# Pairing expert places of unequal size: 128 with 32 and 64 with 32 slots, gathered in one product

## The chip, the core and the metric

The kernel runs on one core of a Trainium2 chip. The figure that counts is the device time of one execution, in microseconds (us). TensorE (PE) does the matrix products; VectorE (DVE) and ScalarE (ACT) read its results from PSUM and work on SBUF; GpSimd (POOL) does little here; SyncE (SP) issues the weight transfers, which 16 DMA engines carry from HBM into SBUF.

## The reference

A batch of 256 tokens of width 1024 passes two transformer blocks in fp32. What matters here is the end of the second one, a mixture of experts with 32 experts, of which each token uses 4:

```python
logits = t @ w_router + b_router                  # [256, 32]
top_val, top_idx = lax.top_k(logits, 4)
gate_w = softmax(top_val)
# for every expert e, over the tokens that chose it:
hb = xb @ w_exp_in[e] + b_exp_in[e]               # 1024 -> 2048
g  = minimum(hb[:, :1024], 7.0);  u = clip(hb[:, 1024:], -7.0, 7.0)
a  = g * sigmoid(1.702 * g) * (u + 1.0)
y_e = a @ w_exp_out[e] + b_exp_out[e]             # 1024 -> 1024
# y = sum over a token's experts of gate_w * y_e; out = layer_norm(ALPHA * h + y)
```

One expert has 3 x 1024 x 1024 fp32 weights, 12.6 MB; all 32 have 403 MB, and every one of them is read once.

## The kernel before

Up to 515 us of the profiled span the kernel does the first block, the attention of the second and the router. After that come the experts. They are worked off one after the other in 32 *places*. A place has a fixed number of token slots (128, 64 or 32, `SLOTS`, L27, read by `caps`), and on the chip the experts are sorted by the number of their tokens, so that the fullest get the places of 128 (`_places`, L1350). Experts 0 and 1 always take places 0 and 1, so that their weights can be fetched before the sort is known (`FIXED`). There are 4 places of 128 slots, 14 of 64 and 14 of 32.

Weights come in *tiles* of 2 MB, six to a place, four of the first matrix and two of the second. `Stream.ahead` (L61 to L73) issues them on SP's queue in the order of the places. A tile goes into one of nine buffers (`ring` 3, `halves` 3, `ring2`, `ring3`, `more4`), so SP waits with a tile until PE has read the tile nine before it. Transfers of one queue land in their order.

For each place (the loop at L1121), `hidden` multiplies the gathered tokens by the first matrix in four blocks (f = 0 to 3). The tokens are the stationary operand, the 512 weight columns stream past; where a place has 64 or 32 slots, two or four such products stand side by side in the array. `gated` turns a block round (by `ident`, or for 32 slots by `fold`, which adds up the four parts) and applies the activation on DVE and ACT. `out_rows` multiplies by the second matrix, `weigh` scales by the gate, and `scatter` adds the rows to the tokens' sums, which stay in four PSUM banks (`acc`).

Tokens are gathered for two places at a time: `gather(r0)` runs in pieces beside the odd place ahead of the pair (`todo`, L1124). `one_hots` makes, for both places and both halves of the tokens, a matrix of 128 columns that holds a one where a token sits in a slot, repeated 128/c times; the product of the tokens `hn` (stationary, 128 x 128) with the 2c columns of both places gives `xs` transposed. Both places of a pair have the same c. DVE copies the columns of the first place from PSUM, ACT those of the second, into one `xs` tile each, from three rotating buffers. A second small product (L1042) fetches gate and token number of every slot.

`sort_experts` runs in steps between blocks; `SORT` says at which (place, block). A scheduler sets the order on every engine from its own estimate of durations; the program's order is a preference only, apart from the stretches under `manual_schedule`.

Of the kernel before, what the change touches and what calls it, by code (L numbers as in the profile page):

```python
# [9 lines left out]
F32 = mybir.dt.float32  # L10
# [9 lines left out]
D = 1024  # L20
# [3 lines left out]
E = 32  # L24
K4 = 4
FIXED = 2
SLOTS = (64, 32, 32, 128, 32, 32, 128, 32, 32, 64, 64, 64, 64, 64, 64, 32)  # L27
RING = 3
HALVES = 3
TAIL = 7  # L30
SORT = ((0, 2), (0, 3), (3, 1), (18, 1), (20, 1))
NPRE = 11 + 4 + 3 * NU + 20 + 4 + 4
ALPHA = 2.0 ** 0.25
LAM_INIT = 0.2
# [89 lines left out]

def caps(r):

    return SLOTS[r // 2]


def build(nc, tc, ctx, a, dbg=None):  # L130
    V, A, T, G = nc.vector, nc.scalar, nc.tensor, nc.gpsimd
# [216 lines left out]
    with tc.manual_schedule(engines={ACT, DVE, mybir.EngineType.Pool}):  # L348
        for c in range(2):
# [5 lines left out]
            start = ws.cut_in(1024 * c + 512, 1024 * c + 1024)  # L355
# [13 lines left out]
    for c in range(2):  # L369
        p = proj_t(ps, ws.next(), xh, xl, step=8 if c else 4)  # L370
        if c == 0:
            r0 = []
# [13 lines left out]
    p = proj_t(ps, w, xh, xl, nm=1)  # L386
    V.tensor_tensor(ka, p[:, 0, :], rt, op=OP.mult)
    p = proj_n(ps, w, xh, xl, c0=128, cols=128)
# [24 lines left out]
    for nm in ("q", "k"):  # L413
        eo = []
        for i in range(2):
            p = proj_t(ps, ws.next(), xh, xl)
# [26 lines left out]
    for c in range(2):  # L443
        p = proj_n(ps, ws.next(), xh, xl)
# [65 lines left out]
    for c in range(2):  # L510
        p = proj_n(ps, ws.next(), xh, xl)
# [4 lines left out]
    for t in range(2):  # L516
        for h in range(4):
            i = t * 4 + h
# [48 lines left out]
    tmp, r = weighed(0, rowf, "r1")  # L567
    r1.append(r)
    summed(0, tmp)
    tmp, r = weighed(1, rowf, "r1")  # L570
# [70 lines left out]
    for t in range(2):  # L641
# [3 lines left out]
        tmp, r = weighed(t, row1, "r3")  # L645
# [21 lines left out]
    oh = act.tile([128, 8, 256], F32R, name="ah")  # L667
# [60 lines left out]
    for g in range(2):  # L728
        at = attention_pt(ps, w1, sa, (4 * g, 4 * g + 2))
        v_n(vB, g)  # L730
        b = ps.tile([128, 2, 2, 128], F32, name="b")
# [38 lines left out]
    mo = pool(ctx, "mo")  # L770
    hn = mo.tile([128, 2, D], F32, name="hn")
    iota = mo.tile([128, 264], F32, name="iota")
# [8 lines left out]
    gtok = mo.tile([128, 2, E, 2], F32, name="gtok")  # L781
# [29 lines left out]
    for c in range(2):  # L811
        wa, wb = ws.next(), ws.next()
        for mm in range(2):
            m = 4 * c + 2 * mm
# [30 lines left out]
    oneh = rp.tile([128, 2, K4, E], F32, name="oneh")  # L845
# [21 lines left out]

    def one_hots(r0, pos):

        c = caps(r0)  # L870
        oh = mo.tile([128, 2, 2, 128 // c, c], F32, name="oneh")
        for t in range(2):
            for i in range(2):
                last = V.tensor_scalar(oh[:, t, i], iota[:, None, 1:c + 1].to_broadcast([128, 128 // c, c]),
                                       pos[:, t, r0 + i:r0 + i + 1], None, op0=OP.is_equal)
        return oh, last

# [2 lines left out]
    for t in range(2):  # L880
# [7 lines left out]
        for k0 in (0, 4):  # L888
            p = ps.tile([128, 4, 128], F32, name="b")
# [11 lines left out]
        b = ps.tile([128, E], F32, name="b")  # L901
# [7 lines left out]
    last = chosen(1)  # L909
    for t in range(2):  # L910
        show(f"logits{t}", logits[:, t, :])
    b = ps.tile([128, 2, E], F32, name="b")
# [26 lines left out]
    em = pool(ctx, "em", 4, space=PSUM)  # L939
# [5 lines left out]
    scr = [acc[t][n] for t in range(2) for n in range(2)]  # L945

    def sort_experts():

        sp = mo
        b = scr[0][:, 0:2 * E].rearrange("p (i e) -> p i e", i=2)  # L950
        for i, (x, y) in enumerate(((sel, ones), (ones, sel))):
            for t in range(2):
                T.matmul(b[0:E, i, :], x[:, t, :] if i == 0 else x[:, 0:E], y[:, 0:E] if i == 0 else y[:, t, :],
                         start=t == 0, stop=t == 1)
        cn = sp.tile([E, E], F32, name="cn")
        V.tensor_copy(cn, b[0:E, 0, :])

        places = ep.tile([128, 128], F32, name="places", bufs=1)
        nc.gpsimd.dma_start(places, a["places"])
        bw = ep.tile([128, 512], F32, name="xs", bufs=3)  # L960
        nc.gpsimd.dma_start(bw, a["bin"])
        key = ep.tile([E, 7, E], F32, name="key", bufs=1)
        V.tensor_scalar(key[:, 0, :], b[0:E, 0, :], float(E), sortc[:, 0:1], op0=OP.mult, op1=OP.add)
        V.scalar_tensor_tensor(key[:, 1, :], b[0:E, 1, :], float(E), sortc[:, 2:2 + E], op0=OP.mult, op1=OP.add)
        V.tensor_tensor(key[:, 2:6, :], key[:, 0:1, :].to_broadcast([E, 4, E]), key[:, 1:2, :].to_broadcast([E, 4, E]),
                        op=OP.is_gt)
        b = scr[1][:, 0:2]
        T.matmul(b, key[:, 2:6, :].rearrange("p a e -> p (a e)"), ones[0:E, 0:2], start=True, stop=True)
        rank = sp.tile([128, 1], F32, name="rank")
        V.tensor_copy(rank, b[:, 0:1])  # L970
        perm = sp.tile([128, 4 * E], F32, name="perm")
        V.tensor_scalar(perm, places, rank, None, op0=OP.is_equal)
        V.tensor_copy(key[:, 6, :], sortc[:, 1:2].to_broadcast([E, E]))
        b = scr[2][0:E, 0:2 * E].rearrange("p (i e) -> p i e", i=2)
        T.matmul(b[:, 0, :], key[:, 6, :], perm[0:E, 0:E], start=True, stop=True)
        T.matmul(b[:, 1, :], cn, perm[0:E, 0:E], start=True, stop=True)
        V.tensor_copy(ids, b[:, 0, :])
        V.tensor_tensor(cn, b[:, 1, :], sortc[:, 2 + E:2 + 2 * E], op=OP.subtract)
        V.tensor_scalar(over, cn, 0.0, None, op0=OP.max)
        V.tensor_reduce(most, over, axis=AX.X, op=OP.max)  # L980
        b = scr[3][:, 0:128]
        T.transpose(b, pg.rearrange("p j t e -> p (j t e)"), ident)
        pgt = ep.tile([128, 128], F32, name="pgt", bufs=1)
        V.tensor_copy(pgt, b)
        b = scr[0][:, 0:4 * E].rearrange("p (j t e) -> p j t e", j=2, t=2)
        T.matmul(b.rearrange("p j t e -> p (j t e)"), pgt, perm, start=True, stop=True)
        V.tensor_copy(posm[:, :, FIXED:], b[:, 0, :, FIXED:])
        V.tensor_copy(gtok[:, :, FIXED:, 0], b[:, 1, :, FIXED:])
        yield
        b = em.tile([128, 4, 4, E], F32, name="m")  # L990
        for m in range(4):
            T.matmul(b[:, m].rearrange("p f e -> p (f e)"), bw[:, m * 128:(m + 1) * 128], perm, start=True, stop=True)
        for j in range(2):
            for i in range(2):
                V.tensor_scalar(bexp[:, FIXED:, :, j, i].rearrange("p e f -> p f e"), b[:, 2 * j + i, :, FIXED:],
                                float(j), None, op0=OP.add)
        yield

        bw = ep.tile([128, D], F32, name="xs", bufs=3)
        for t in range(2):  # L1000
            nc.gpsimd.dma_start(bw[64 + t * E:64 + (t + 1) * E, :], a["bout"])
        for n in range(2):
            for t in range(2):
                r = slice(64 + t * E, 64 + (t + 1) * E)
                T.matmul(acc[t][n], pgt[r, :], bw[r, n * 512:(n + 1) * 512], start=False, stop=False,
                         skip_group_check=True)

        for t in range(2):
            yield
            for n in range(2):  # L1010
                T.matmul(acc[t][n], aid, hn[:, t, n * 512:(n + 1) * 512], start=False, stop=False,
                         skip_group_check=True)
# [4 lines left out]
    ep = pool(ex2, "ep", 2)  # L1017

    def gather(r0):

        c = caps(r0)
        oh, _ = first if r0 == 0 else one_hots(r0, posm)
        xs = [ep.tile([128, 8, c], F32, name="xs", bufs=3) for _ in range(2)]
        for i in range(2):
            slots_of[r0 + i] = [xs[i]]
        per = min(8, 256 // c)
        for at, k0 in enumerate(range(0, 8, per)):
            b = (em.tile([128, 512], F32, name="m") if r0 else scr[at])[:, 0:per * 2 * c]  # L1030
            b = b.rearrange("p (k i c) -> p k i c", k=per, i=2)
            for kk in range(per):
                f = slice((k0 + kk) * 128, (k0 + kk + 1) * 128)
                for t in range(2):
                    T.matmul(b[:, kk], hn[:, t, f], oh[:, t, :, 0, :], start=t == 0, stop=t == 1)  # L1035
            for i in range(2):
                (A.copy if i else V.tensor_copy)(xs[i][:, k0:k0 + per], b[:, :, i, :])
            yield
        for i in range(2):
            b = em.tile([128, 2], F32, name="m")  # L1040
            for t in range(2):
                T.matmul(b, oh[:, t, i].rearrange("p d c -> p (d c)"), gtok[:, t, r0 + i, :],  # L1042
                         start=t == 0, stop=t == 1)
            gs = ep.tile([128, 2], F32, name="gs", bufs=5)
            V.tensor_copy(gs, b)
            V.tensor_scalar(gs[:, 0:1], gs[:, 0:1], 0.5, None, op0=OP.mult)
            so = ep.tile([128, 256], F32R, name="so", bufs=3)
            V.tensor_scalar(so, iota[:, 0:S], gs[:, 1:2], None, op0=OP.is_equal)
            slots_of[r0 + i] += gs[:, 0:1], so
# [65 lines left out]
    slots_of = {}  # L1115
# [5 lines left out]
    for r in range(E):  # L1121
        xs = slots_of[r][0]
# [304 lines left out]
```

## Time and profile before

| | us |
|---|---|
| timed runs of the kernel before | 1485.1, 1479.3, 1487.65 (median 1485.1) |
| the profiled execution, its own time | 1477.87 |
| its span | 1476.1 |
| granted TensorE clock, mean over the span | 0.978 |
| busy: PE, DVE, ACT | 1394.0 (94%), 657.4 (45%), 433.6 (29%) |

The page cuts the span into 40 slices of 36.9 us and shows a digit of busy share for each engine, the granted clock of TensorE, the share of the DMA engines and the bytes moved. PE's busy time is the time from the start of a product to its modelled end, so products that run beside one another or wait in the array for the one ahead count in full; PE at 9 in every slice does not mean that PE sets the pace there. The chain of waits on the page reaches back only to 1464 us, to the branch ahead of the final normalization, and tells nothing about the experts. For those one goes to the stretches, to the order of PE's work in time, and to what SP waits for.

### The profile page before, as it was taken

How to read it: one execution, taken by the hardware profiler on the slowest of the kernel's cores; microseconds unless marked ns; L12 is line 12 of the kernel's file. 1: busy time of each engine (PE TensorE's matmuls, PEld its weight loads, DVE VectorE, ACT ScalarE, POOL GpSimd, SP SyncE). 2: the span in 40 equal slices, each digit the busy share in tenths (PEclk: the TensorE clock that was granted, in tenths of full speed). 3: DMA queues.
4: the chain of work that ended last, by engine and by line, in shares of the span. 5: the costliest groups of instructions: out<-in, count | busy, mean ns of one | idle time of the engine just before them, and what ended most of it. 6: DMA issues, size and time to landing. Idle time of an engine off the chain costs nothing. (4 is left out here: it accounts for less than half of the span.)

```text
span 1476.1 us, 21068 instructions
## 1 busy us (share of the span) xinstructions
PE 1394.0 (94%) x8401; PEld 882.1 (60%) x8402; DVE 657.4 (45%) x1622; ACT 433.6 (29%) x819; POOL 36.7 (2%) x54
## 2 busy tenths in 40 slices
PE   7998999989999899999999899998999999999984
PEld 7988999979999744544545444454343443443431
DVE  5868977866667533222123221232332333233313
ACT  4535655544565212121112211122111111111111
POOL 1001000010001100000000000000000000000000
PEclk9999999999999999899999999999999999999987
DMA  8435545535435989999989999899999999999995
GB/s 350 172 129 184 215 172 199 203 137 200 179 142 197 392 328 365 427 427 426 427 349 418 426 427 426 349 417 427 426 426 428 426 427 426 427 426 427 426 427 213
DMA packets 38008, 495.15 MB, mean 335 GB/s; under 512 B 4561, under 2 KB 4881, under 8 KB 8593
## 3 DMA queue, kind: packets, MB, share of 16 engines
q1 hardware_dynamic: 35424, 486.69, 79.8%
q0 software_dynamic: 2192, 6.88, 1.4%
q8 instruction: 68, 1.11, 0.3%
q14 instruction: 36, 0.29, 0.1%
q10 hardware_dynamic: 288, 0.18, 0.0%
HBM read 492.68 MB, written 1.05 MB: 334 GB/s over the span
## 5 line engine op out<-in xcount | busy, mean ns | idle before, releaser
L1060 PE MATMUL m<-w,xs 128*64 128x512 f32 (+2 forms) x1392 | 315.2, 611 | 10.3 <-DMA w<-in_wexp_dram 10.3
L1077 DVE TENSOR_TENSOR gu<-m,bexp 128x256 f32<-128x256 f32 (+2 forms) x128 | 51.1, 399 | 457.2 <-PE m L1074 310.9
L1060 PEld LDWEIGHTS m<-w,xs 128*64 128x64 f32 (+2 forms) x1392 | 102.3, 136 | 167.9 <-issue 157.3
L1063 ACT COPY hs<-m 128x512 f32<-128x512 f32 x128 | 74.9, 585 | 416.0 <-PE m L1060 416.0
L232 PE MATMUL b<-ah,wh 128*128 128x256 f32 x1552 | 194.3, 282 | 1.4 <-ACT wh L83 1.4
L232 PEld LDWEIGHTS b<-ah,wh 128*128 128x128 f32 x1552 | 187.6, 191 | 3.3 <-ACT wh L83 1.8
L105 DVE TENSOR_TENSOR wh<-w,wh 128x1024 fp32r<-128x1024 f32 (+1 forms) x152 | 174.2, 1180 | 31.7 <-ACT wh L104 31.7
L104 ACT ACTIVATE wh<-w 128x1024 fp32r<-128x1024 f32 (+1 forms) x154 | 148.7, 1019 | 79.8 <-PE b L232 43.4
L1097 PE MATMUL m<-w,ea 128*32 128x512 f32 (+2 forms) x672 | 141.6, 614 | 9.3 <-DMA w<-in_wexp_dram 6.3
L1060 PE MATMUL m<-wh,xs 128*32 128x512 f32 (+2 forms) x656 | 121.4, 597 | 8.4 <-DMA wh<-in_wexp_dram 8.1
L205 DVE SCALAR_TENSOR_TENSOR one<-m,gs,one 128x512 fp32r<-128x512 f32 x64 | 46.8, 749 | 129.1 <-ACT one L204 127.7
L1084 ACT ACTIVATE th<-gu 128x128 f32<-128x128 f32 (+2 forms) x128 | 38.4, 300 | 215.3 <-DVE gu L1082 215.3
L232 PE MATMUL b<-al,wh 128*128 128x256 f32 x776 | 99.4, 280 | 0.0
L232 PEld LDWEIGHTS b<-al,wh 128*128 128x128 f32 x776 | 94.5, 190 | 0.0
L1097 PE MATMUL m<-wh,ea 128*64 128x512 f32 (+2 forms) x352 | 85.5, 627 | 4.9 <-DMA wh<-in_wexp_dram 4.1
L1097 PEld LDWEIGHTS m<-w,ea 128*32 128x32 f32 (+2 forms) x672 | 40.6, 129 | 78.4 <-issue 55.9
L1112 PE MATMUL acc<-one,so 128*128 128x512 f32 x256 | 77.5, 423 | 9.7 <-ACT one L204 8.6
L1072 PEld LDWEIGHTS m<-fold,hs 128*128 128x128 f32 x448 | 56.6, 196 | 48.0 <-issue 35.9
L1060 PEld LDWEIGHTS m<-wh,xs 128*32 128x32 f32 (+2 forms) x656 | 35.5, 124 | 72.4 <-issue 66.0
L1112 PEld LDWEIGHTS acc<-one,so 128*128 128x128 f32 x256 | 43.0, 188 | 50.0 <-ACT one L204 29.0
L1035 PE MATMUL m<-oneh,hn 128*128 128x64 f32 (+2 forms) x480 | 69.0, 299 | 0.0
L204 ACT ACTIVATE one<-m,gs 128x512 fp32r<-128x512 f32 x64 | 42.5, 686 | 82.1 <-PE m L1097 82.0
(370 smaller groups left out, 1384.5 us busy)
## 6 DMA issues: line engine op xcount, KB each, us to landing
w<-in_wexp_dram SPq DMA_DIRECT2D x128, 2048.0 KB, 37.4
wh<-in_wexp_dram SPq DMA_DIRECT2D x63, 2048.0 KB, 37.5
w<-in_wpre_dram SPq DMA_DIRECT2D x37, 2048.0 KB, 7.9
w<-in_wpre_dram SPq DMA_DIRECT2D x4, 512.0 KB, 7.9
w<-in_wexp_dram SPq DMA_DIRECT2D x4, 512.0 KB, 30.3
tab<-in_tab_dram SPq DMA_DIRECT2D x1, 1152.0 KB, 10.0
xn<-in_x_dram SPq DMA_DIRECT2D x2, 512.0 KB, 5.0
ra<-in_rowv_dram POOLq DMA_DIRECT2D x2, 512.0 KB, 7.2
```

The source lines that it names most:

```text
L104: self.nc.scalar.activation(h[:, c], t[:, c], AF.Copy)
L105: self.nc.vector.tensor_tensor(l[:, c], t[:, c], h[:, c].bitcast(F32), op=OP.subtract)
L204: return (A.activation(hi, src, AF.Copy, scale=scale), V.scalar_tensor_tensor(lo, src, scale, hi.bitcast(F32), op0=OP.mult, op1=OP.subtract))
L205: V.scalar_tensor_tensor(lo, src, scale, hi.bitcast(F32), op0=OP.mult, op1=OP.subtract))
L232: T.matmul(p[:, m, :], x[:, k, c], y[:, k, :], start=i == m == k == 0, stop=i == 2 and k == nk - 1, skip_group_check=True)
L1035: T.matmul(b[:, kk], hn[:, t, f], oh[:, t, :, 0, :], start=t == 0, stop=t == 1)
L1060: T.matmul(b[g * c:(g + 1) * c], xs[:, k, :], w[:, kk, :], start=k < n, stop=k >= 8 - n, skip_group_check=True)
L1063: A.copy(h, b)
L1072: T.matmul(p[:, j, :], h[:, j * 128:(j + 1) * 128], fold, start=True, stop=True)
L1077: V.tensor_tensor(both, p[:, :, 0:c], bexp[:, r, f].rearrange("p j i -> p (j i)")[:, :, None].to_broadcast([128, 4, c]), op=OP.add)
L1097: T.matmul(ys[n][g * c:(g + 1) * c], ac[:, kk, :], w[:, kk, n * 512:(n + 1) * 512], start=(j == kk == 0) if c == 128 else j < 64 // c, sto ...
L1112: T.matmul(acc[t][n], so[:, t * 128:(t + 1) * 128], y[:, n, :], start=first and y is yh, stop=last and y is yl, skip_group_check=True)
```

## The change

`SLOTS` now has one entry for each place. The list of sizes is the same (4 of 128, 14 of 64, 14 of 32), in another order:

```
before  64,64  32,32  32,32  128,128  32,32  32,32  128,128  32,32  32,32  six times 64,64  32,32
after   64,64  32,64  32,64  128,32  64,32  128,32  64,32  128,32  64,32  128,32  64,64  five times 64,32
```

Since the two places of a pair may differ, `one_hots` writes each place's matrix with its own c, and the gather takes the last c0 columns of the first and the first c1 of the second, which lie next to each other, as one streaming operand of c0 + c1 columns. Both places share one tile `xs`, which alternates between two names (`xs0`, `xs1`) with a buffer each. A PSUM bank is filled with as many 128-row blocks as fit (`per`: five of 96 columns, four of 128, three of 160) and copied by one instruction, on DVE and ACT in turn. In `sort_experts` the two bias tiles take these names, and the fetch and the use of the second one become two steps of `SORT`, at place 2, block 1 and block 3, where one step stood at place 3, block 1.

```diff
-SLOTS = (64, 32, 32, 128, 32, 32, 128, 32, 32, 64, 64, 64, 64, 64, 64, 32)
+SLOTS = ((64, 64, 32, 64, 32, 64) + 3 * (128, 32, 64, 32) + (128, 32, 64, 64) + 5 * (64, 32))
-SORT = ((0, 2), (0, 3), (3, 1), (18, 1), (20, 1))
+SORT = ((0, 2), (0, 3), (2, 1), (2, 3), (18, 1), (20, 1))
 def caps(r):
-    return SLOTS[r // 2]
+    return SLOTS[r]
...
-        c = caps(r0)
-        oh = mo.tile([128, 2, 2, 128 // c, c], F32, name="oneh")
+        oh = mo.tile([128, 2, 2, 128], F32, name="oneh")
         for t in range(2):
             for i in range(2):
-                last = V.tensor_scalar(oh[:, t, i], iota[:, None, 1:c + 1].to_broadcast([128, 128 // c, c]),
+                c = caps(r0 + i)
+                last = V.tensor_scalar(oh[:, t, i].rearrange("p (d c) -> p d c", c=c),
+                                       iota[:, None, 1:c + 1].to_broadcast([128, 128 // c, c]),
...
-        bw = ep.tile([128, D], F32, name="xs", bufs=3)
+        bw = ep.tile([128, D], F32, name="xs0", bufs=1)
         for t in range(2):
             nc.gpsimd.dma_start(bw[64 + t * E:64 + (t + 1) * E, :], a["bout"])
+        yield
...
-        c = caps(r0)
+        c0, c1 = caps(r0), caps(r0 + 1)
+        c = c0 + c1
-        xs = [ep.tile([128, 8, c], F32, name="xs", bufs=3) for _ in range(2)]
-        for i in range(2):
-            slots_of[r0 + i] = [xs[i]]
-        per = min(8, 256 // c)
+        xs = ep.tile([128, 8, c], F32, name=f"xs{r0 // 2 % 2}", bufs=1)
+        slots_of[r0], slots_of[r0 + 1] = [xs[:, :, 0:c0]], [xs[:, :, c0:]]
+        per = min(8, 512 // c)
         for at, k0 in enumerate(range(0, 8, per)):
...
-                    T.matmul(b[:, kk], hn[:, t, f], oh[:, t, :, 0, :], start=t == 0, stop=t == 1)
-            for i in range(2):
-                (A.copy if i else V.tensor_copy)(xs[i][:, k0:k0 + per], b[:, :, i, :])
+                    T.matmul(b[:, kk], hn[:, t, f], oh[:, t].rearrange("p i c -> p (i c)")[:, 128 - c0:128 + c1],
+                             start=t == 0, stop=t == 1)
+            (A.copy if at % 2 else V.tensor_copy)(xs[:, k0:k0 + n], b)
```

The lines of the changed kernel stand one or two further down than those of before (the product of `hidden` is L1060 before and L1061 after, that of `gather` L1035 and L1037). Two places in the order of PE show what moves.

First the place after the first 128. In the kernel before, PE goes from place 6 (128 slots) to place 7, also 128; `w`, `wh` are weight tiles, `xs` the gathered tokens, `ea` the activations, `oneh` the one-hot columns. An x8 counts instructions of the program; the trace has two records for each such fp32 product.

```order
L1097 MATMUL m<-wh_6336,ea 128x512 x4
L1060 MATMUL m<-wh_6392,xs 128x512 x8
L1097 MATMUL m<-wh_6336,ea 128x512 x4
L1060 MATMUL m<-w,xs 128x512 x8
L1074 MATMUL m<-ident,hs 128x128
```

In the changed kernel place 7 has 32 slots:

```order
L1098 MATMUL m<-wh_6340,ea 128x512 x4
L1061 MATMUL m<-wh_6406,xs_6290 32x512 x8
L1098 MATMUL m<-wh_6340,ea 128x512 x4
L1061 MATMUL m<-w,xs_6290 32x512 x8
L1073 MATMUL m<-fold,hs 128x32 x4
```

The blocks stand in the same order; those behind the 128 are now products of 32 slots, and the next 128 comes three places later.

Second, the gather for places 2 and 3, on PE beside place 1. Before:

```order
L1035 MATMUL m<-oneh,hn 128x64 x9
L1060 MATMUL m<-w,xs 64x512 x8
L1074 MATMUL m<-ident,hs 128x128 x4
L1042 MATMUL m<-gtok,oneh 128x2 x4
L1060 MATMUL m<-w_5361,xs 64x512 x8
L1074 MATMUL m<-ident,hs 128x128 x4
```

After:

```order
L1037 MATMUL m<-oneh,hn 128x96 x3
L1061 MATMUL m<-w,xs_5297 64x512 x8
L1075 MATMUL m<-ident,hs 128x128 x4
L1037 MATMUL m<-oneh,hn 128x96 x6
L1061 MATMUL m<-w_5358,xs_5297 64x512 x8
L1075 MATMUL m<-ident,hs 128x128 x4
L1044 MATMUL m<-gtok,oneh 128x2 x4
```

There are still 16 products for the pair. They are 96 columns wide where they were 64, and stand in two groups (of ten and six) with a block of `hidden` between them, where they stood in one.

## Rows read from the trace of the kernel before

**Rows 1.** The page: granted clock and bytes moved, in 40 slices of 36.9 us.
```profile
PEclk9999999999999999899999999999999999999987
GB/s 350 172 129 184 215 172 199 203 137 200 179 142 197 392 328 365 427 427 426 427 349 418 426 427 426 349 417 427 426 426 428 426 427 426 427 426 427 426 427 213
```
**Rows 2.** Stretches: us, busy time of each engine (x instructions), clock, DMA share, GB/s.
```profile
548.00:584.00 36.00, 36.00 (x206) 16.43 (x202) 11.22 (x40) 7.45 (x16) 1.00 (x2) 1.00 0.93 365
606.00:617.00 11.00, 11.00 (x50) 7.50 (x48) 0.42 (x1) 0.37 (x1) 0.00 (x0) 0.53 1.01 427
740.00:800.00 60.00, 60.00 (x319) 29.67 (x317) 16.23 (x56) 10.72 (x23) 0.00 (x0) 1.00 0.90 374
764.00:776.00 12.00, 12.00 (x62) 4.71 (x60) 2.98 (x8) 2.94 (x6) 0.00 (x0) 1.00 0.50 182
932.00:992.00 60.00, 60.00 (x359) 30.55 (x362) 20.14 (x78) 11.60 (x26) 0.00 (x0) 1.00 0.90 372
1052.00:1400.00 348.00, 336.81 (x1658) 141.30 (x1656) 113.39 (x377) 62.17 (x129) 0.00 (x0) 1.00 1.01 427
```
**Rows 3.** What SP's queue waited for from 744 to 780 us: total, times, longest.
```profile
SPq L69 <- PE m L1060: 22.9, 3, 12.2
SPq L69 <- PE m L1097: 17.6, 2, 10.8
```
**Rows 4.** PE in order of time, place 6: start, us, line, product [idle before].
```profile
691.25 7.03 PE L1060 MATMUL m<-w,xs 128*128 128x512 f32 x16
698.12 0.60 PE L1074 MATMUL m<-ident,hs 128*128 128x128 f32 x4
698.55 7.03 PE L1060 MATMUL m<-w,xs 128*128 128x512 f32 x16
```
**Rows 5.** PE in order of time, places 24 and 25, from scatter to scatter.
```profile
1224.70 2.46 PE L1112 MATMUL acc<-one,so 128*128 128x512 f32 x8
...
1243.78 1.94 PE L1097 MATMUL m<-wh,ea 128*64 128x512 f32 x8 [0.66 <-DMA wh<-in_wexp_dram]
...
1248.69 3.65 PE L1097 MATMUL m<-wh,ea 128*64 128x512 f32 x16 [0.52 <-DMA wh<-in_wexp_dram]
1252.27 2.44 PE L1112 MATMUL acc<-one,so 128*128 128x512 f32 x8
...
1283.11 2.22 PE L1112 MATMUL acc<-one,so 128*128 128x512 f32 x7
```
**Rows 6.** PE in order of time: first products of places 2 to 5, and one wait.
```profile
576.38 1.92 PE L1060 MATMUL m<-w,xs 128*32 128x512 f32 x16
...
595.28 1.49 PE L1060 MATMUL m<-w,xs 128*32 128x512 f32 x11
...
630.42 1.92 PE L1060 MATMUL m<-wh,xs 128*32 128x512 f32 x16
...
648.66 1.92 PE L1060 MATMUL m<-w,xs 128*32 128x512 f32 x16
651.59 1.92 PE L1060 MATMUL m<-wh,xs 128*32 128x512 f32 x16 [1.00 <-DMA wh<-in_wexp_dram]
```
**Rows 7.** PE in order of time: gathers of 64 and 128 columns, and a slow stretch.
```profile
606.86 7.09 PE L1035 MATMUL m<-oneh,hn 128*128 128x64 f32 x32
613.88 3.30 PE L1060 MATMUL m<-w,xs 128*32 128x512 f32 x16
...
736.08 3.68 PE L1035 MATMUL m<-oneh,hn 128*128 128x64 f32 x32
...
1268.52 1.95 PE L1035 MATMUL m<-oneh,hn 128*128 128x128 f32 x16
```
**Rows 8.** Groups by shape: out<-in xcount | busy us, mean ns | idle before.
```profile
L1063 ACT COPY hs<-m 128x512 f32<-128x512 f32 x128 | 74.9, 585 | 416.0 <-PE m L1060 416.0
L1035 PE MATMUL m<-oneh,hn 128*128 128x256 f32 x64 | 15.8, 389 | 0.0
L1077 DVE TENSOR_TENSOR gu<-m,bexp 128x512 f32<-128x512 f32 x16 | 11.1, 692 | 108.4 <-PE m L1074 108.4
```

More of the change, by code (lines that the diff above doesn't have):

```diff
@@ L959, in sort_experts @@
         nc.gpsimd.dma_start(places, a["places"])
-        bw = ep.tile([128, 512], F32, name="xs", bufs=3)
+        bw = ep.tile([128, 512], F32, name="xs1", bufs=1)
         nc.gpsimd.dma_start(bw, a["bin"])
@@ L1019, in gather @@
     def gather(r0):
-        c = caps(r0)
+        c0, c1 = caps(r0), caps(r0 + 1)
+        c = c0 + c1
         oh, _ = first if r0 == 0 else one_hots(r0, posm)
-        xs = [ep.tile([128, 8, c], F32, name="xs", bufs=3) for _ in range(2)]
-        for i in range(2):
-            slots_of[r0 + i] = [xs[i]]
-        per = min(8, 256 // c)
+        xs = ep.tile([128, 8, c], F32, name=f"xs{r0 // 2 % 2}", bufs=1)
+        slots_of[r0], slots_of[r0 + 1] = [xs[:, :, 0:c0]], [xs[:, :, c0:]]
+        per = min(8, 512 // c)
         for at, k0 in enumerate(range(0, 8, per)):
-            b = (em.tile([128, 512], F32, name="m") if r0 else scr[at])[:, 0:per * 2 * c]
-            b = b.rearrange("p (k i c) -> p k i c", k=per, i=2)
-            for kk in range(per):
+            n = min(per, 8 - k0)
+            b = (em.tile([128, 512], F32, name="m") if r0 else scr[at])[:, 0:n * c].rearrange("p (k c) -> p k c", k=n)
+            for kk in range(n):
                 f = slice((k0 + kk) * 128, (k0 + kk + 1) * 128)
                 for t in range(2):
-                    T.matmul(b[:, kk], hn[:, t, f], oh[:, t, :, 0, :], start=t == 0, stop=t == 1)
-            for i in range(2):
-                (A.copy if i else V.tensor_copy)(xs[i][:, k0:k0 + per], b[:, :, i, :])
+                    T.matmul(b[:, kk], hn[:, t, f], oh[:, t].rearrange("p i c -> p (i c)")[:, 128 - c0:128 + c1],
+                             start=t == 0, stop=t == 1)
+            (A.copy if at % 2 else V.tensor_copy)(xs[:, k0:k0 + n], b)
             yield
@@ L1041, in gather @@
             for t in range(2):
-                T.matmul(b, oh[:, t, i].rearrange("p d c -> p (d c)"), gtok[:, t, r0 + i, :],
-                         start=t == 0, stop=t == 1)
+                T.matmul(b, oh[:, t, i], gtok[:, t, r0 + i, :], start=t == 0, stop=t == 1)
             gs = ep.tile([128, 2], F32, name="gs", bufs=5)
```

## The prediction

> **What bounds the kernel now.** I read the slices of the page first. In the experts, from slice 17 on, the transfers run at 426 to 428 GB/s, and a few slices fall to 349 [rows 1]. That is the first thing to see: a flat ceiling with dents. 403 MB at that rate are 943 us, which is about the length of the stage, so the weight stream is the pace. The stretches confirm it: 427 GB/s over 348 us from 1052 us, and in two stretches of 60 us only 374 and 372 [rows 2]. One place, 12.58 MB, takes 12.58/0.427 = 29.5 us, one tile 4.9 us.
>
> The dents: (1 - 374/427) x 60 = 7.4 us of the stream are lost between 740 and 800 us, and (1 - 372/427) x 60 = 7.7 us between 932 and 992 [rows 2]; together 15.1 us. In the first of them SP waits for products, up to 12.2 us at a time, not for earlier transfers [rows 3]: all nine buffers are full, and PE is late in reading. Both dents follow the two pairs of 128-slot places (6 and 7, 12 and 13).
>
> Now PE's pace, place by place.
> - 128 slots: a block of `hidden` with no other work in it takes 698.12 - 691.25 = 6.87 us, the turn 0.43 us [rows 4]. `out_rows` has half as many products of the same shape. So 6 x 6.87 + 4 x 0.43 + 2.4 for the scatter [rows 5] = 45.3 us.
> - 64 slots: place 24, scatter to scatter, 27.57 us, less 1.18 us of waiting for weights = 26.4 us. Place 25, with a gather of 128 columns beside it, takes 30.8 us; the gather costs 4.4 us [rows 5].
> - 32 slots: place 4, 648.66 - 630.42 = 18.2 us [rows 6].
>
> Against 29.5 us, a 128 puts PE back by 15.8 us, a 64 brings 3.1 and a 32 11.3 us forward. Let the *lag* be the time by which PE starts a place after its first tile has landed. At 651.59 us PE waits for the second tile of place 5 [rows 6], which has just landed; the first landed 4.9 us earlier, at 646.7 us, so the lag of place 5 is 2.0 us. It is about 1 us at place 6, since place 5 with its gather is short of 29.5 us. Two 128s and the gather beside them (64 columns, 4.2 us by the rows below) cost 2 x 45.3 + 4.2 = 94.8 us against 59.0 us: at the end of place 7 the lag would be 37 us, and 7.4 us of it became a dent. The buffers hold about 29.5 us.
>
> **The change, part by part.** *Order of the places.* A cycle of 128, 32, 64, 32 costs PE 45.3 + 18.2 + 26.4 + 18.2 us and two gathers. The stream needs 117.9 us for it.
>
> *The gathers.* 64 columns take 3.68 us for 32 records, 128 columns 1.95 us for 16 [rows 7]: the same for each product. So 96, between the two, costs as much; with the small products behind it the gather is 4.2 us at 64 columns and 4.4 at 128, and I take 4.4. 256 columns take 7.9 us for 32 records (15.8 us for two pairs) [rows 8]. A pair of 160 columns lies between 3.9 and 7.9 us; I take 4.9 us, a quarter of the way, since 160 is a quarter of the way from 128 to 256. With the small products, 5.4 us. The cycle is then 108.1 + 4.4 + 5.4 = 117.9 us, level with the stream; 3 us more if 160 costs as much as 256, 1 us less if as little as 128.
>
> *The start of the run of cycles.* Backwards from place 5: place 4 took 18.2 us, so its lag was 2.0 + 29.5 - 18.2 = 13.3 us; place 3 took 35.1 us: 7.7 us; place 2 took 18.9 us [rows 6], and (1 - 365/427) x 36 = 5.2 us of the stream were lost beside the sort [rows 2]: 23.5 us. All this is untouched by the change. Place 3's 35.1 us contain 12.7 us beyond 18.2 + 4.2: the bias products of the sort and a stretch at half clock. I leave these 12.7 us in, whatever place they now fall in. Places 2 to 5 are then 18.9 + 12.7 + (26.4 + 4.4) + 18.2 + (26.4 + 5.4) = 112.4 us against 117.9 + 5.2, and the lag at place 6 is 23.5 + 112.4 - 123.1 = 12.8 us. After the 128 it is 12.8 + 45.3 - 29.5 = 28.6 us, just under the 29.5 us at which the stream stops. The three places behind it take it down to 12.8 us again, four times over. So both dents go, 15.1 us, and with a margin of 1 us something comes back: I take 2 us in all, between 0 and 10 us (a cycle 3 us over the stream four times, less the margin, gives 11).
>
> *The end.* Behind the last cycle come 64, 64 and five pairs of 64, 32: 26.4 + 18.2 + 4.4 = 49.0 us against 59.0 us. The lag is gone after two of them, and the last place has 32 slots in both kernels. The stream sets the end, and its gain is the kernel's.
>
> *Copies.* 58 copies of 256 columns become 36 of 288 to 512. The nearest rows, other reads of 512 columns out of PSUM, take 692 ns on DVE and 585 ns on ACT [rows 8]. They are needed one place later, 18 us away, and both engines are busy for less than a third of this stage [rows 2]: nothing. If that cover were gone, 3 x 0.7 us would stand in each pair's gather, at most 2 us a pair. Sharing a buffer between the places takes nothing away, since the tile that is overwritten belongs to the pair before the last one. *Sort.* The second bias fetch and its products come a place earlier, behind the same buffer; nothing, and if PE waited for the fetch, less than the 18.9 us of place 2, in a lag that would then cost that much at place 6. One transpose moves ahead of the first product: under 1 us, and the stream is stopped there by full buffers only later.
>
> *A rule against it.* From 606 to 617 us the granted clock is 0.53, that is mostly the lower level (1.2 GHz); PE was at work all the time [rows 2], on narrow products and on bias products with 32 rows. The Trainium skill (TensorE: Matmul & The Clock Gate, "HAM oscillation — how this bites in real kernels") says that a kernel whose matmuls wait for transfers between bursts falls back to the slow clock burst by burst. By it the last ten places, with 10 us of waiting in each pair, would run at half clock: a pair would take 2 x 49 = 98 us instead of 59, and the end would come 5 x 39 = 195 us later, near 1664 us. This case's trace does not bear that out: from slice 18 to slice 38 the clock digit is 9 (0.9 or more) throughout, though pairs of 32 wait longer than pairs of 64, 32 will [rows 1].
>
> The sum: 1477.9 - 15.1 + 2 = 1464.8 us for an execution like the profiled one. The median of the timed runs lies 7.2 us above that execution and the lowest 1.4 us; I carry 4 us, and predict 1469 us.
>
> **The rivals.** *The dents come back smaller.* PE's cycle is level with the stream by my sum, and 2 to 3 us more in each would fill the buffers behind every 128. For it: the margin of 1 us, and the unknown price of 160 columns. Against it: the 12.7 us at place 3 need not all return. Gain 3 to 9 us; profile 1472, predicted time 1476 us.
>
> *The stream is not on the path.* The weights come earlier, and PE, which now has no pause from place 6 to place 21, sets the end itself. For it: PE is at 9 in nearly every slice. Against it: from 1222 us PE waits 0.66 and 0.52 us for tiles [rows 5], so it is level with the stream twelve places before the end, and the new order leaves 10 us more in each of the last pairs. No change: 1482 us.
>
> *Slower: the half clock.* At 606 us the gather takes 7.09 us instead of 3.68 and a block 3.30 us instead of 1.92 [rows 6, 7]: 4.8 us for one stretch. If it came in both 32s of a cycle, where narrow products, scatter and gather meet, a cycle would be 9.6 us longer; four of them, less the 1 us of margin, stop the stream for 37 us against 15.1 us removed. It turns against the kernel at 4 us a cycle. With one stretch a cycle: 18 us against 15, with two, 22 us lost. I price it between them, 12 us on 1477.9 + 4: 1494 us. (The rule's own case, 1664 us, gets 0.01 of this rival's chance.) For it: the stretch came with PE busy. Against it: behind slice 17 the clock digit stays at 9 through ten places of 32 slots, up to slice 38 [rows 1].
>
> **How the numbers follow.** The forecast (gain 9 to 16 us) 0.62, the smaller dents 0.20, no change 0.10, the half clock 0.08. What a measurement of this kernel can tell from no change is 0.5%, 7.4 us of 1485.1. Faster: 0.62, and two fifths of the smaller dents, 0.08, make 0.70. Slower: the half clock and a little of no change, 0.10. The rest, 0.20, is the same. The range for eight in ten: from 1459 us (15.1 us off the profiled execution with nothing coming back is 1462.8, less 4 us for the spread of the runs) to 1486 us (no change, with the median's excess).
>
> **What would show it.** Right: slices at 426 from 600 us on, SP waiting for transfers and not 10 us for products behind a 128, and pairs of 96 columns at 3.7 to 4 us for 32 records. Smaller dents would show as 10 us waits of SP at places 8, 12, 16 and 20. The stream is not on the path if PE has no waits for weights after 1250 us. The half clock is in the clock row. My lags are wrong if PE waits for weights between places 6 and 20.

## The result, and the profile after

The changed kernel takes 1467.0 us (median of 4 runs, 1466.1 to 1467.3), the kernel before 1482.4 us (median of 4, 1479.3 to 1487.7) beside it. The ratio is 0.989 with an interval of 0.986 to 0.993. The profiled execution of the changed kernel took 1467.0 us, with a span of 1465.2 us; that of before had 1477.9 and 1476.1.

The page of the changed kernel has the same two lines as [rows 1], clock and bytes in 40 slices, here of 36.6 us; the third line is from its list of transfers (number of issues, KB each, median us from issue to landing).

```profile
PEclk9999999999999989999999999999999999999997
GB/s 351 175 93 179 225 208 174 178 178 203 162 146 150 393 313 373 425 426 427 427 426 428 426 428 426 426 426 427 426 427 427 426 428 424 428 427 426 425 428 204
w<-in_wexp_dram SPq DMA_DIRECT2D x128, 2048.0 KB, 27.3
```

The four slices of 349, 418, 349 and 417 are gone: from slice 17 to the last but one all stand between 424 and 428. The stretches that answer to [rows 2], with the same columns:

```profile
548.00:584.00 36.00, 36.00 (x202) 16.82 (x201) 13.15 (x47) 6.15 (x13) 1.01 (x2) 1.00 0.93 371
606.00:617.00 11.00, 11.00 (x66) 5.99 (x60) 3.85 (x9) 2.64 (x5) 0.00 (x0) 1.00 1.01 426
740.00:800.00 60.00, 58.70 (x380) 28.31 (x380) 20.25 (x78) 12.50 (x27) 0.00 (x0) 1.00 1.01 427
932.00:992.00 60.00, 58.75 (x277) 29.32 (x275) 17.33 (x55) 9.84 (x20) 0.00 (x0) 1.00 1.01 427
1052.00:1400.00 348.00, 325.58 (x1778) 146.34 (x1776) 101.32 (x350) 60.80 (x126) 0.00 (x0) 0.98 1.01 427
```

740 to 800 and 932 to 992 went from 374 and 372 to 427 GB/s. The stretch at 606 us, which had the clock at 0.53, has it at 1.00.

Next, PE in order of time (start, us, line, product, idle time before it and what ended it): the first products of places 2, 6, 7, 8 and 10, and two waits in the last places.

```profile
580.23 1.92 PE L1061 MATMUL m<-w,xs 128*32 128x512 f32 x16
...
686.27 13.89 PE L1061 MATMUL m<-w,xs 128*128 128x512 f32 x32
...
725.89 1.92 PE L1061 MATMUL m<-wh,xs 128*32 128x512 f32 x16
...
754.94 3.65 PE L1061 MATMUL m<-w,xs 128*64 128x512 f32 x16
...
804.90 5.31 PE L1061 MATMUL m<-wh,xs 128*128 128x512 f32 x12
...
1401.39 3.65 PE L1061 MATMUL m<-w,xs 128*64 128x512 f32 x16 [0.67 <-DMA w<-in_wexp_dram]
...
1425.90 1.92 PE L1061 MATMUL m<-w,xs 128*32 128x512 f32 x16 [1.93 <-DMA w<-in_wexp_dram]
```

A cycle of 128, 32, 64, 32 took 804.90 - 686.27 = 118.6 us, the second as long, the third 120.3 us. With the landing times of the first tiles, which the trace records, the lags come out at 6.7 us at place 6 and 6.2, 7.2 and 8.4 us at places 10, 14 and 18. From place 20, where it is 20.8 us, the lag falls to 0.3 us at place 26; from there on PE waits for weights, as in the two last rows. The stream sets the end.

The clean measure of the gain is the time from the first product of place 0 to the end of the span. The two rows are that product, before and after, each from its own trace.

```profile
522.90 3.65 PE L1060 MATMUL m<-w,xs 128*64 128x512 f32 x16
```

```profile
526.86 3.65 PE L1061 MATMUL m<-w,xs 128*64 128x512 f32 x16
```

Before: 1476.1 - 522.9 = 953.2 us. After: 1465.2 - 526.9 = 938.3 us. The experts became 14.9 us shorter, and the two dents had held 15.1 us.

### The profile page after: what moved, and what is told of

It is laid out like the page before. It is cut to its first block, busy times and chain, and to the rows that moved or that the text cites. A ratio compares the mean times of both kernels' runs of the same rounds, so it can differ in the third digit from the quotient of the medians.

```text
span 1465.2 us, 21035 instructions
## 1 busy us (share of the span) xinstructions
PE 1386.9 (95%) x8401; PEld 878.4 (60%) x8402; DVE 659.4 (45%) x1613; ACT 429.9 (29%) x806; POOL 36.7 (3%) x54
## 5 line engine op out<-in xcount | busy, mean ns | idle before, releaser
L1061 PE MATMUL m<-w,xs 128*64 128x512 f32 (+2 forms) x1392 | 301.7, 600 | 10.7 <-DMA w<-in_wexp_dram 10.7
L1061 PEld LDWEIGHTS m<-w,xs 128*64 128x64 f32 (+2 forms) x1392 | 96.6, 133 | 167.9 <-issue 160.7
L1098 PE MATMUL m<-w,ea 128*32 128x512 f32 (+2 forms) x672 | 136.9, 625 | 8.2 <-DMA w<-in_wexp_dram 6.5
L1061 PE MATMUL m<-wh,xs 128*32 128x512 f32 (+2 forms) x656 | 127.8, 597 | 4.5 <-DMA wh<-in_wexp_dram 4.5
L1073 PEld LDWEIGHTS m<-fold,hs 128*128 128x128 f32 x448 | 55.6, 194 | 47.1 <-issue 36.9
L1061 PEld LDWEIGHTS m<-wh,xs 128*32 128x32 f32 (+2 forms) x656 | 39.2, 128 | 71.2 <-issue 68.3
L1037 PE MATMUL m<-oneh,hn 128*128 128x96 f32 (+2 forms) x480 | 64.2, 283 | 0.0
## 6 DMA issues: line engine op xcount, KB each, us to landing
w<-in_wexp_dram SPq DMA_DIRECT2D x128, 2048.0 KB, 27.3
```

What stands on the lines that cost most here:

```text
L1037: T.matmul(b[:, kk], hn[:, t, f], oh[:, t].rearrange("p i c -> p (i c)")[:, 128 - c0:128 + c1], start=t == 0, stop=t == 1)
L1061: T.matmul(b[g * c:(g + 1) * c], xs[:, k, :], w[:, kk, :], start=k < n, stop=k >= 8 - n, skip_group_check=True)
L1073: T.matmul(p[:, j, :], h[:, j * 128:(j + 1) * 128], fold, start=True, stop=True)
L1098: T.matmul(ys[n][g * c:(g + 1) * c], ac[:, kk, :], w[:, kk, n * 512:(n + 1) * 512], start=(j == kk == 0) if c == 128 else j < 64 // c, sto ...
```

## The experiments

Two questions were open. Is it the order of the places that brings the 15 us, or the joint gather with its fewer copies? And does the lag, measured against what the buffers hold, explain the dents, or would any order that mixes large with small do? Below, "stage" is the time from place 0's first product to the end of the span, 953.2 us before and 938.3 us after. In a SLOTS edit the removed line is that of the changed kernel.

**The joint gather with the old order (e1_old_order).**

```diff
-SLOTS = ((64, 64, 32, 64, 32, 64) + 3 * (128, 32, 64, 32) + (128, 32, 64, 64) + 5 * (64, 32))
+SLOTS = tuple(c for c in (64, 32, 32, 128, 32, 32, 128, 32, 32, 64, 64, 64, 64, 64, 64, 32) for _ in range(2))
```

> The joint product and the shared tile stay, the places stand in the order of the kernel before (pairs of equal size). Theory (the order of the places alone decides, through the lag of PE behind the weight stream and the nine buffers): both dents come back, 7 to 8 us of the stream lost at 740-800 us and again at 932-992 us, time near 1482 us. Rival (the gather in one product with fewer copies is what gains): no dents worth the name, 1467 us.

Measured: 1479.8 us against 1480.0 for the kernel before, ratio 0.9996 (0.9977 to 1.0015); the stage is 953.1 us. The two stretches in its trace:

```profile
740.00:800.00 60.00, 60.00 (x320) 29.80 (x318) 16.69 (x56) 10.06 (x21) 0.00 (x0) 1.00 0.90 373
932.00:992.00 60.00, 60.00 (x359) 30.56 (x362) 20.39 (x78) 11.23 (x25) 0.00 (x0) 1.00 0.90 372
```

Both dents are back, to within 1 GB/s. In the old order the rewritten gather is worth nothing, and so are its fewer copies; the gain comes with the new order. Whether that order needs the joint gather for it is the next question.

**The new order, each pair gathered in two products (e2_two_products).**

```diff
-                for t in range(2):
-                    T.matmul(b[:, kk], hn[:, t, f], oh[:, t].rearrange("p i c -> p (i c)")[:, 128 - c0:128 + c1],
-                             start=t == 0, stop=t == 1)
+                for x, y in ((128 - c0, 128), (128, 128 + c1)):
+                    for t in range(2):
+                        T.matmul(b[:, kk, x - 128 + c0:y - 128 + c0], hn[:, t, f], oh[:, t].rearrange("p i c -> p (i c)")[:, x:y],
+                                 start=t == 0, stop=t == 1)
```

> The order of the changed kernel, but each place of a pair is gathered by a product of its own, 32 products for a pair where there were 16. Theory: 32 products of 64 records take 64 x 0.115 = 7.4 us where 96 columns take 3.7 and 160 about 4.9, so a cycle of four places is 6 us over the stream; from a lag at the end of the first 128 of 22.5 + 6 = 28.7 us against 29.5 us that the buffers hold, the second, third and fourth 128 stop the stream for about 5, 6 and 6 us: 1467 + 17 = 1484 us, SP waiting for PE behind places 10, 14 and 18. Rival (PE's work is hidden behind the stream as long as the order is mixed): 1467 to 1470 us.

Measured: 1520.2 us, ratio to before 1.024 (1.019 to 1.028). Slower than before, as expected, but by 36 us more than expected. Its clock row, its first gather, its stretches and two moments with the clock low:

```profile
PEclk9999999999999799999999999999999996996998
...
520.86 13.89 PE L1038 MATMUL acc<-oneh,hn 128*128 128x64 f32 x64 [0.73 <-DVE oneh L874]
...
524.00:584.00 60.00, 60.00 (x310) 35.03 (x310) 16.76 (x63) 7.61 (x15) 0.00 (x0) 0.87 0.71 285
560.00:860.00 300.00, 296.49 (x1610) 147.61 (x1607) 85.41 (x289) 50.32 (x103) 1.01 (x2) 0.99 0.99 417
860.00:1160.00 300.00, 294.52 (x1583) 150.53 (x1583) 82.08 (x275) 49.12 (x100) 0.00 (x0) 0.99 0.94 391
1160.00:1460.00 300.00, 298.62 (x1612) 143.81 (x1612) 82.81 (x293) 48.98 (x103) 0.00 (x0) 0.89 0.99 414
...
1256.00:1280.00 24.00, 24.00 (x111) 14.92 (x111) 4.30 (x21) 2.08 (x5) 0.00 (x0) 0.50 0.93 384
1375.00:1402.00 27.00, 27.00 (x127) 16.35 (x126) 5.34 (x26) 2.34 (x6) 0.00 (x0) 0.51 1.01 426
```

The first gather takes 13.9 us where the changed kernel's takes 6.4, and place 0 starts 9 us later (the clock is at its lower level beside both, in e2 from 516 to 539 us at 0.50). Then the stream, which waits for buffers, loses 7.0, 25.3 and 9.1 us in the three long stretches (each (1 - GB/s / 427) x 300): 41.4 us, where the theory had 17. It had no term for the later start and none for the clock. At 1256 and 1375 us the clock is at its lower level for 24 and 27 us, with PE busy all the time. And all PE waited for from 560 to 1510 us were these two (total, times, longest):

```profile
PE acc L1114 <- ACT one L204: 8.7, 11, 0.8
PE m L1099 <- DVE ea L1090: 2.5, 6, 0.4
```

No transfer is among them: here PE sets the end, with a lag of 24 us still at the last place. So the new order with a product for each place loses; with the joint product, which keeps the gather at the price of one, it gains. How much of the 58.6 us between the two spans belongs to the doubled products and how much to the clock I can't separate, since the parts overlap.

**The four 128s, each with a 32, one behind the other (e3_wide_in_a_row).**

```diff
-SLOTS = ((64, 64, 32, 64, 32, 64) + 3 * (128, 32, 64, 32) + (128, 32, 64, 64) + 5 * (64, 32))
+SLOTS = ((64, 64, 32, 64, 32, 64) + 4 * (128, 32) + 3 * (64, 32) + (64, 64) + 5 * (64, 32))
```

> The changed kernel with the four pairs of 128 and 32 in a row, the three pairs of 64 and 32 behind them; all sizes and products are the same. Theory: each such pair costs PE 45.3 + 18.2 + 4.4 = 67.9 us against 59.0 us of the stream, the lag at the end of the 128s is 22.5, 31.4 and so on, capacity 29.5 us: the stream stops for 2, 9 and 9 us, 20 us in all, 1487 us. Rival (any mixing of sizes within a pair is enough): 1467 us.

Measured: 1492.7 us (1485.7 to 1496.2), ratio 1.007 (1.005 to 1.009); the stage is 1490.8 - 524.3 = 966.5 us, 28.2 longer than that of the changed kernel. The stretch and the page's row of bytes:

```profile
800.00:1000.00 200.00, 196.44 (x940) 97.48 (x940) 53.57 (x177) 32.00 (x65) 0.00 (x0) 0.97 0.92 371
...
GB/s 347 170 120 189 215 170 203 204 127 198 178 170 187 377 331 400 426 426 427 428 427 406 356 349 358 350 427 426 426 426 427 426 427 427 427 427 427 426 427 202
```

The pairs hold the same mix, yet (1 - 371/427) x 200 = 26.2 us are lost, more than in the kernel before. A pair of 128, 32 costs PE 68.9 us with its gather, against 59.0 us of the stream, and four of them in a row add up: the lags at the four 128s are 6.5, 17.2, 28.6 and 33.5 us, where the changed kernel has 6.7, 6.2, 7.2 and 8.4. (Two short stretches at half clock, at 819 and 890 us, add to it; they may be the 6 us beyond the expected 20.) It is the running sum that decides, not the mix within a pair.

**The changed kernel again, and with eight buffers in place of nine, in both kernels (e4_after_again, e5_eight_buffers_after, e6_eight_buffers_before).** e4 has no edit; e5 and e6 have this one, on the changed kernel and on the kernel before:

```diff
-    ws.free += ws.halves + [(pool(ctx, "more4"), "w")]
+    ws.free += ws.halves
```

> The changed kernel itself, as the yardstick for the runs beside it: 1467 us, ratio to the kernel before 0.99. Rival (a difference of chips or days): anything else.

> The changed kernel with eight weight buffers instead of nine. Theory: the lag that stops the stream falls from 29.5 to 24.6 us, and the largest lag at the end of a 128 is 6.7 + 45.3 - 29.5 = 22.5 us in the first three cycles and 24 us in the last: still no dents in the middle; only the start, where all buffers are full while the router works, loses one more tile, 5 us: 1472 us. Rival (any loss of buffering costs, the order has no margin): 1480 us or more.

> The kernel before with eight weight buffers instead of nine. Theory: one tile more at the start, and 4.9 us more in each of the two dents: 1480 + 5 + 10 = 1495 us, so that the distance to the changed kernel grows from 13 to 23 us. Rival (the dents are of another kind, such as the place's own latency): 1485 us, the same distance as with nine.

Measured, beside the kernel before at 1481.0 us: e4 1467.3 us, ratio 0.991 (0.989 to 0.993), stage 1463.4 - 525.0 = 938.4 us; e5 three runs of 1467.9 to 1471.9 us, median 1469.9 (a fourth took 3526 us, for a reason that nothing here shows, and is no part of the ratio), ratio 0.993 (0.990 to 0.996), stage 943.5 us; e6 1497.4 us, ratio 1.011 (1.009 to 1.014), stage 971.3 us. The two stretches, in e5 and then in e6:

```profile
740.00:800.00 60.00, 58.18 (x372) 26.55 (x371) 20.83 (x82) 12.12 (x26) 0.00 (x0) 1.00 1.01 426
932.00:992.00 60.00, 58.75 (x282) 29.05 (x282) 17.35 (x55) 9.83 (x20) 0.00 (x0) 1.00 1.01 427
```

```profile
740.00:800.00 60.00, 60.00 (x308) 29.96 (x306) 17.02 (x55) 10.95 (x22) 0.00 (x0) 1.00 0.79 317
932.00:992.00 60.00, 60.00 (x311) 30.68 (x310) 17.98 (x60) 11.24 (x23) 0.00 (x0) 1.00 0.84 332
```

With one buffer less the old order's dents grow to 15.5 and 13.3 us, 13.7 us more than the 15.1 of before, where 4.9 us in each were expected. The rest comes from the lags: at places 6 and 12 they were 4.0 and 1.5 us in e6 and 1.1 us each before, and 4.9 + 2.9 and 4.9 + 0.4 are the 8.1 and 5.6 us by which the dents grew, to within 0.3 us. The new order shows no dent. Its stage still grows by 5.1 us, about one tile of 4.9 us that can't be fetched ahead of place 0 (when place 0 begins, nine tiles have been issued in e4, eight in e5); with the same 4.9 us, the 18.1 us by which the old order's stage grows are 13.7 + 4.9 to within half a microsecond. So the distance between the orders goes from 14 to about 27 us (23 expected), as buffers that fill up require.

**Place 1 with 32 slots and place 3 with 64 (e7_place1_with_32).**

```diff
-SLOTS = ((64, 64, 32, 64, 32, 64) + 3 * (128, 32, 64, 32) + (128, 32, 64, 64) + 5 * (64, 32))
+SLOTS = ((64, 32, 64, 32, 64, 32) + 3 * (128, 32, 64, 32) + (128, 32, 64, 64) + 5 * (64, 32))
```

> The changed kernel with 32 slots at place 1 (its expert has 19 tokens with these inputs), 13 places of 64 and 15 of 32. Theory: PE reads the tiles of place 1 8 us earlier, so the stream, which stands still beside the sort for want of buffers, loses 2 to 4 us less between 548 and 584 us; nothing else changes, since the stream sets the end: 1464 us. Rival (PE's total work counts, 8 us less of it): 1459 us. Rival (the loss there belongs to the sort's own waits): 1467 us.

Measured: 1465.1 us (1464.4 to 1466.2), ratio 0.989 (0.987 to 0.991); 2.2 us below e4, which ran beside it with runs of 1465.1 to 1468.8, so the two overlap. The stage is 1462.6 - 525.9 = 936.7 us, 1.7 us shorter than e4's. The stretch next to the sort, in e4 and then here:

```profile
548.00:584.00 36.00, 36.00 (x208) 16.78 (x206) 12.47 (x43) 6.15 (x13) 1.01 (x2) 1.00 0.93 372
```

```profile
548.00:584.00 36.00, 36.00 (x239) 16.82 (x236) 11.33 (x42) 7.89 (x16) 1.01 (x2) 1.00 1.01 404
```

The loss there is (1 - 404/427) x 36 = 1.9 us in place of 4.6. These 2.7 us less agree with the theory, and about 2 us of them came out; that small a difference is not shown beyond doubt by four runs of each. The median is the lowest of the versions tried. Place 1 is always expert 1, which has 19 tokens here; with more than 32, its other tokens would need the kernel's branch for overfull places, and what that costs wasn't tried.

## Why the prediction was right, point by point

**Dents (15.1 us): right.** Both went, and the stage is 14.9 us shorter. e1 shows that the order does it, e2 that it loses without the joint product, e3, e5 and e6 that the dents are a matter of buffers filling up.

**Residual (2 us, from a margin of 1 us): too large, it was nothing.** The lag at place 6 was 6.7 us where the sum said 12.8. The step that failed is places 2 to 5: they took 686.27 - 580.23 = 106.0 us, not 112.4. I had left 12.7 us of place 3 in, "whatever place they now fall in"; part of them was the stretch at half clock, and that did not come. Place 18 had the largest lag of the four 128s; by the sum its end is at 8.4 + 15.8 = 24.2 us, so 5 us were free under the 29.5 us. In e5, with eight buffers (29.5 - 4.9 = 24.6 us), the lag at place 18 was 5.2 us, which makes 21.0 us at its end: it fits, and e5 has no dent.

**Gathers: right.** The groups by shape in the changed kernel, where the joint products stand apart:

```profile
L1037 PE MATMUL m<-oneh,hn 128*128 128x96 f32 x320 | 40.0, 276 | 0.0
L1037 PE MATMUL m<-oneh,hn 128*128 128x160 f32 x128 | 20.1, 305 | 0.0
```

96 columns: 40.0/320 x 32 = 4.0 us a pair, where I had said 3.7 to 4. 160 columns: 20.1/128 x 32 = 5.0 us, 4.9 taken. The cycle, 117.9 us by the sum, measured 118.6 to 120.3 us.

**Copies (nothing): right.** e1 has the old order with the joint gather's copies and its time did not move; and after the change no copy stands in what PE waited for from 560 to 1200 us (total, times, longest):

```profile
PE acc L1113 <- ACT one L204: 6.2, 8, 0.8
PE m L1098 <- DVE ea L1089: 1.7, 4, 0.4
```

**Sort (nothing): not shown by itself.** The stream's loss beside it is 4.7 us, 5.2 before, but the first product of place 0 came 4.0 us later in this execution. Under the new order with the joint gather it stood between 522.6 us (e5) and 526.9 us, under the old one at 522.9 to 523.0 us (before, e1, e6). Whether the order costs a part of that, or it is scatter, stays open.

**The 4 us carried from the profiled execution to the timed runs: wrong in kind.** After, the profiled execution lies at the median. 1477.9 - 14.9 + 4.0 = 1467.0 us: I had put 2 us of residual and 4 us for the timed runs on top of the gain, and neither came; the 4.0 us of the later start stand in their place. The total, 1467.0 us against 1469, is nearer the forecast than its terms: that closeness is partly luck; the 15 us of the dents is not.

**One of the signs was badly chosen.** I named "SP waiting for transfers and not 10 us for products behind a 128" as a sign. SP's waits over the whole span (total, times, longest), after:

```profile
SPq L69 <- PE m L1061: 391.7, 92, 10.4
SPq L69 <- PE m L1098: 213.6, 49, 10.5
```

and before:

```profile
SPq L69 <- PE m L1060: 225.1, 62, 14.7
SPq L69 <- PE m L1097: 134.0, 36, 13.6
```

They went up from 359 to 605 us and still reach 10.5 us, though the slices of GB/s show no dent from slice 17 on. SP's waits that are put down to earlier transfers fell meanwhile from 433 to 171 us, so the sum of both hardly moved (792 and 777 us): SP waits for a free buffer in either kernel, and what changed is which of the two came last. Issue to landing is 27.3 us at the median, 5 to 6 tiles of 4.9 us (37.4 us before): SP waits behind a queue that still has work. A wait of SP stops the stream only when it outlasts what is queued. The slices of GB/s were the sign that told.

**The rivals.** Smaller dents: refuted by the slices. The stream not on the path: refuted by the waits for weights from place 26 on, while e2 shows what it looks like. Half clock: it did not come in the cycles: the mean clock from 620 to 1260 us is 1.00 (last row of this document). From 1212 us on it came for a few us at a time: 0.98 from 1052 to 1400 us, with 348 - 325.6 = 22.4 us of pauses in it. Two of the stretches with a fall in them, and three rows of the last pairs:

```profile
1205.00:1225.00 20.00, 19.16 (x130) 9.28 (x124) 6.30 (x28) 3.61 (x8) 0.00 (x0) 0.91 1.01 428
1375.00:1390.00 15.00, 13.34 (x86) 6.67 (x85) 3.80 (x21) 1.94 (x6) 0.00 (x0) 0.77 1.01 427
...
1381.80 1.93 PE L1098 MATMUL m<-w,ea 128*32 128x512 f32 x8 [1.10 <-DMA w<-in_wexp_dram]
...
1430.80 1.92 PE L1061 MATMUL m<-w,xs 128*32 128x512 f32 x16 [1.97 <-DMA w<-in_wexp_dram]
...
1435.80 3.19 PE L1061 MATMUL m<-w,xs 128*32 128x512 f32 x16 [2.07 <-DMA w<-in_wexp_dram]
```

Behind a wait of 1.97 us 16 records took 1.92 us, behind the next, of 2.07 us, the same 16 took 3.19; the eight at 1381 us, behind 1.10 us, took 1.93 us where eight such take 1.06 at a clock of 1.00 (at 646 us). The fall beside 1212 us came without such a wait. The rule of the Trainium skill that I had weighed (TensorE: Matmul & The Clock Gate, "HAM oscillation — how this bites in real kernels"), by which waits for transfers between bursts bring the slow clock, is thus borne out in part: the clock fell behind some of these waits and not behind others, and never for a whole pair, as my 195 us had assumed. The falls cost nothing here, since PE waits for the stream behind them. In e2 the clock fell for long with PE busy 24.00 of 24 us. So the mechanism that I had priced as the slower rival exists; it came in e2, which has twice the gather products, and not in the cycles of this change.

## What to carry to other kernels

Where a steady stream feeds places of unequal cost, add up cost minus the stream's time per place, place by place: the stream stops where that sum passes what the buffers hold, and the order of the places is a way to keep it below that costs nothing as long as the work itself stays as it was. Two small products that share their stationary side are worth joining when a product's price does not fall with its columns. To see whether a queue's wait matters, look at the bytes moved, not at the wait.

## What the runs showed of the hardware

A gather product of 96 columns costs as much as one of 64: one piece of such a gather took 2.14 us for 18 records after, and 3.68 us for 32 before [rows 7], that is 0.12 us a record either way.

```profile
736.31 2.14 PE L1037 MATMUL m<-oneh,hn 128*128 128x96 f32 x18
```

Narrower ones are not cheaper either. In e2 a run of 38 records, about half of them with 64 and half with 32 columns, took 4.33 us at a clock of 1.00, 0.114 us each:

```profile
757.03 4.33 PE L1038 MATMUL m<-oneh,hn 128*128 128x64 f32 x38
```

In e2 the clock fell where narrow products followed each other without a pause. The stretch at 1256 us begins inside such a gather, beside a place of 32 slots: 16 records of the same shape take 1.90 us before it and 3.64 us behind it. In the changed kernel it also fell behind pauses, as the rows at 1381 and 1435 us above show. What makes it fall is not settled by these rows.

```profile
1249.84 1.90 PE L1062 MATMUL m<-wh,xs 128*32 128x512 f32 x16
...
1252.58 5.45 PE L1038 MATMUL m<-oneh,hn 128*128 128x64 f32 x40
1257.96 3.64 PE L1062 MATMUL m<-wh,xs 128*32 128x512 f32 x16
```

Over 640 us, the transfers of one core held 427 GB/s without a dent, PE, DVE and ACT working beside them:

```profile
620.00:1260.00 640.00, 630.38 (x3262) 293.82 (x3264) 192.55 (x649) 113.78 (x234) 0.00 (x0) 1.00 1.01 427
```
